# Two decoder layers on one core: the mixers' and the cross attention's input projections get their activations held still and 512 weight columns moved, with the results turned on TensorE

## The chip, the core and the metric

The kernel runs on one core of a Trainium2 chip. The core has a matrix engine (TensorE, "PE" in the profile), a vector engine (VectorE, "DVE"), an activation engine (ScalarE, "ACT"), a general engine (GpSimd, "POOL"), and a synchronisation engine (SyncE, "SP") that here issues nearly all loads. The metric is the time of one execution on the device, in microseconds (us), as the median of several runs.

## The reference

One sequence of 256 tokens, 2048 wide, goes through two decoder layers and a final RMSNorm. All inputs and weights are fp32. Layer 0 has a hybrid mixer, layer 1 a state-space mixer ("ssd"); each is followed by a cross attention into 256 memory tokens and a SwiGLU feed-forward layer 5632 wide. Every part is pre-normed and added to the residual.

```python
def rmsnorm(x, w):
    return x * rsqrt(mean(x * x, -1) + NORM_EPS) * w

def hybrid(p, x):                       # layer 0: one projection 2048 -> 8208, split by columns
    q, f, i, g, qb, kb, vb, gb, beta, a = split(x @ hy_w_in)   # 6 x 1024 of HGRN2/DeltaNet q,k,v, 2 gates, 2 x 8
    o_a = hgrn2_chunked(silu(q), 1 - fg, i, log(fg))           # fg = lb + (1 - lb) * sigmoid(f)
    conv = silu(causal_depthwise_conv([qb, kb, vb], taps=4))
    o_b = gated_delta_chunked(l2norm(q), l2norm(k), v, sigmoid(beta), -exp(a_log) * softplus(a + dt_bias))
    return concat(gated_head_norm(o_a), gated_head_norm(o_b)) @ hy_w_out

def ssd(p, x):                          # layer 1: 2048 -> 10304
    z, xBC, dt = split(x @ ssd_w_in)                           # 4096, 4096 + 2 * 1024, 64
    x, B, C = split(silu(causal_depthwise_conv(xBC, taps=4) + b))
    y = scan over chunks(x * dt, B, C, exp(-exp(a_log) * dt)) + D * x
    return rmsnorm(y * silu(z)) @ ssd_w_out

def xattn(p, x, mem):                   # 4 heads of 128
    q, k, v = x @ xa_wq, norm(mem) @ xa_wk, norm(mem) @ xa_wv
    return softmax(q @ k.T / sqrt(128)) @ v @ xa_wo

def ffn(p, x):
    return (silu(x @ w_gate) * (x @ w_up)) @ w_down
```

The gated delta rule is computed by chunks of 128 tokens here; each chunk and head needs the inverse of a unit lower-triangular matrix.

## The kernel before, in words

**Weights.** Every weight matrix is laid out beforehand as tiles of 128 rows by 1024 numbers (512 KB): two k-tiles of 512 columns. A tile is loaded by SP into `wr` (4 buffers), ACT casts it to fp32r as `wh` (line 156), DVE takes the rest `wl` = `wr` - `wh` (line 124). The activations are split in the same way into `u` tiles hi and lo. A product is then three fp32r matmuls: hi by hi, hi by lo, lo by hi (the helper's line 121 is the line of all matmuls). The norm's gain is put on the activations when they are split; its scale per token, r, is put on the result.

**Two forms of a projection.** `xstat` holds a 128x128 piece of the activations still and moves 512 weight columns past it: per k-tile 2 token halves x 3 matmuls, the result has tokens on the partitions, and r is one number per partition. The gates, the feed-forward layers and all output projections have this form (rows "acc<-wh,u" and "acc<-wl,u", 128x512). `wstat` holds a 128x128 piece of the weights still and moves the 256 tokens: per k-tile 4 x 3 matmuls, the result has channels on the partitions, and r must stand along the free axis, spread over all partitions (`row`, tile `rB`); DVE multiplies the accumulator by it (`scaled`). The mixers' q, k, v, f, x, B, C, z, the attention's q and k, and two blocks of 128 columns that hold the small heads (beta, a, dt) have this form (rows "acc<-u,wh" and "acc<-u,wl", 128x256).

**Around them.** PSUM has 4 banks for accumulators ("acc") and 4 for the rest ("mx"). The causal convolution (`conv`, line 390) reads channels by tokens from a padded SBUF tile `raw`: one ACT product, three DVE multiply-adds. A tag "b2" of 4 SBUF buffers serves short-lived tiles: squares, norm temporaries, the steps of the triangular inverse, the head norm.

**The triangular inverse** of a DeltaNet head group (`gdn`, twice, 4 heads each): after the k-by-kq products DVE makes M, POOL's queue writes it to a DRAM scratch and reads its 16x16 blocks back, DVE inverts these in 15 steps, and the results go through the scratch again into X and XT. Then come three block levels by two chunks on PE, each a product with XT, an ACT copy (line 619), products with X and with XT and a DVE subtraction; then the products with v and M, the state products ("w,D"), and the head norm (`head_norm`: ACT squares, a DVE sum and a DVE reciprocal square root, four DVE products and four transposes per chunk).

**Order.** The program is written in the order of the mathematics. A list scheduler of the compiler, which runs a simulated timeline, sets the order of the instructions on each engine; loads marked `later` keep their written place. A buffer that rotates (4 of "b2", 4 of "acc") makes its next writer wait for the last reader of the one that is 4 back.

**Start.** The first norm (N0) has its hi part made by DVE (line 267) and lo part by DVE (line 127); its squares are made by ACT, added by POOL and DVE, summed over partitions with ones on PE, and `row` is made of that. The residual h (4 tiles of 512 KB) is loaded between the two DeltaNet groups.

Of the kernel before, what the change touches and what calls it, by code (L numbers as in the profile page):

```python
# [9 lines left out]
F32 = mybir.dt.float32  # L10
# [8 lines left out]
P = 128  # L19
# [9 lines left out]
for _name, _w in (("norm_mix", 32), ("norm_xattn", 32), ("norm_mem", 32), ("norm_ffn", 32), ("norm_final", 16),  # L29
                  ("lb", 16), ("hgrn_norm", 8), ("gdn_conv", 96), ("gdn_norm", 8),  # L30
                  ("ssd_conv", 192), ("ssd_conv_b", 48), ("ssd_norm", 32), ("ssd_d", 32),
                  ("gdn_a_log", 1), ("gdn_dt_bias", 1), ("ssd_a_log", 1), ("ssd_dt_bias", 1)):
# [13 lines left out]
    "ssd_w_in": ([(0, KT, n, 512) for n in range(0, 8192, 512)] + [(0, KT, n, 256) for n in range(8192, 10240, 256)]  # L46
# [32 lines left out]
def trunk(ctx: ExitStack, tc: tile.TileContext, A: dict, out: bass.AP):  # L79
# [92 lines left out]
    def wstat(W, n0, n, u, k0=0, nk=KT):  # L172

        nt = n // P
        accs = [pa.tile([P, min(2, nt), T], F32, name="acc", tag="acc") for _ in range((nt + 1) // 2)]
        for k, wh, wl in wtiles(W, k0, nk, n0, n):
            xh, xl = u[k // 4][0][:, k % 4, :], u[k // 4][1][:, k % 4, :]
            for c in range(nt):
                o = accs[c // 2][:, c % 2, :]
                sl = slice(c * P, (c + 1) * P)  # L180
                mm(o, wh[:, sl], xh, k == 0 and c % 2 == 0, False)
                mm(o, wh[:, sl], xl, False, False)
                mm(o, wl[:, sl], xh, False, k == nk - 1)
        return accs
# [29 lines left out]
    class SquareSum:  # L214
# [17 lines left out]
        def rows(self, n):  # L232

            rB = cp.tile([P, T], F32, name="rB", tag="rB", bufs=2)
            ps = psb([P, T])
            mm(ps, ones, self.s)
            rsqrt(rB, ps, n)
            return rB

# [9 lines left out]
    class Norm:  # L249


        def __init__(self, gain, load=None, hi=act):
            self.hi = hi
            self.gain = gain
            self.load = load
            self.u = Lazy(self.loaded) if load else []
            self.ss = SquareSum()
            self.rB = self.r = None

        def block(self, nb, src):  # L260
            hi, lo = utiles()
            for c in range(4):
                g = col(self.gain[0], self.gain[1] + nb * 4 + c)
                if self.hi is act:
                    act.activation(hi[:, c], src[:, c], AF.Copy, scale=g)  # L265
                else:
                    dve.tensor_scalar(hi[:, c], src[:, c], g, None, op0=ALU.mult)  # L267
                stt(lo[:, c], src[:, c], g, hi[:, c].bitcast(F32), ALU.mult, ALU.subtract)
            self.u.append((hi, lo))
            self.ss.add(src)  # L270
            return hi, lo

        def loaded(self, nb):
            self.block(nb, self.load(nb))
            if nb == 3 and self.hi is act:
                self.row()
                self.column()
# [789 lines left out]
```

## Time and profile before

| what | value |
| --- | --- |
| median of 3 runs | 2985.55 us (2983.79 to 2987.41) |
| the profiled execution | 2986.46 us, of which the span from first to last instruction is 2984.4 us |
| PE busy | 2948.9 us (99%), 16970 rows |
| DVE busy | 1808.7 us (61%) |
| ACT busy | 1427.8 us (48%) |
| POOL busy | 308.4 us (10%) |
| mean granted clock of PE | 0.996 |

By the names of the weights in the trace the hybrid mixer lies at 0 to about 600 us, its cross attention to 702, the first feed-forward layer to 1440, ssd to 2165, the second cross attention to 2248, and the second feed-forward layer to the end.

A row of a group reads: line, engine, operation, output<-inputs, shape, xcount | busy us, mean ns of one | idle before, and what ended it. A row of the chain of waits reads: start us, duration us, engine, tile and line, xcount. A row of a table by stretches reads: from:to, length, then busy us (xcount) of PE, weight loads, DVE, ACT and POOL, then the granted clock, the DMA share and GB/s. An fp32 matmul that isn't fp32r stands as two rows of the trace; the order's listings below show it as one.

### The profile page before, as it was taken

How to read it: one execution, taken by the hardware profiler on the slowest of the kernel's cores; microseconds unless marked ns; L12 is line 12 of the kernel's file. 1: busy time of each engine (PE TensorE's matmuls, PEld its weight loads, DVE VectorE, ACT ScalarE, POOL GpSimd, SP SyncE). 2: the span in 40 equal slices, each digit the busy share in tenths (PEclk: the TensorE clock that was granted, in tenths of full speed). 3: DMA queues.
4: the chain of work that ended last, by engine and by line, in shares of the span. 5: the costliest groups of instructions: out<-in, count | busy, mean ns of one | idle time of the engine just before them, and what ended most of it. 6: DMA issues, size and time to landing. Idle time of an engine off the chain costs nothing.

```text
span 2984.4 us, 42629 instructions
## 1 busy us (share of the span) xinstructions
PE 2948.9 (99%) x16970; PEld 2594.9 (87%) x16970; DVE 1808.7 (61%) x2284; ACT 1427.8 (48%) x1809; POOL 308.4 (10%) x257
## 2 busy tenths in 40 slices
PE   8999999999999999999999999999999999999998
PEld 8899898898888888888999989998888888888887
DVE  8777587676455445455677746767675454455455
ACT  5445354555443444344555545555555444443344
POOL 2211232020000000000032302322010000000000
PEclk9999999999999999999999999999999999999999
DMA  6554434555655665655545465545655556666654
GB/s 228 189 158 149 157 114 152 186 192 171 189 190 192 191 192 187 196 189 186 170 156 170 154 193 169 163 163 168 190 193 184 190 190 191 191 190 191 195 188 145
DMA packets 152183, 533.66 MB, mean 179 GB/s; under 512 B 16592, under 2 KB 22864, under 8 KB 151984
## 3 DMA queue, kind: packets, MB, share of 16 engines
q1 hardware_dynamic: 150096, 526.08, 54.9%
q0 software_dynamic: 1472, 4.59, 0.6%
q8 instruction: 133, 2.18, 0.3%
q14 instruction: 66, 0.54, 0.1%
q10 hardware_dynamic: 416, 0.27, 0.0%
HBM read 526.42 MB, written 4.46 MB: 178 GB/s over the span
## 4 chain that ended last, share of the span: by engine, by line
PE 92%; DVE 2%; issue 2%; DMA 1%; ACT 1%; POOL 1%; POOLq 0%; DVEq 0%; SPq 0%; ACTq 0%
PE acc L121 85%; PE mx L121 5%; PE mx L302 1%; DVE wl L124 1%; DMA wr<-in_memT 1%; DMA XT<-scratch 0%; POOL tmp L124 0%; DVE tmp L124 0%; ACT wh L156 0%; DMA scratch<-b 0%; PE mx L902 0%; DVE b L124 0%; DVE u L267 0%; DVE u L127 0%; ACT u L265 0%
## 5 line engine op out<-in xcount | busy, mean ns | idle before, releaser
L124 DVE TENSOR_TENSOR wl<-wr,wh 128x1024 fp32r<-128x1024 f32 x980 | 1240.7, 1268 | 1026.8 <-ACT wh L156 1024.3
L121 PE MATMUL acc<-wh,u 128*128 128x512 f32 (+1 forms) x5728 | 1755.8, 387 | 0.0
L156 ACT CAST wh<-wr 128x1024 fp32r<-128x1024 f32 x980 | 1029.6, 1052 | 1314.3 <-PE acc L121 1203.9
L121 PEld LDWEIGHTS acc<-wh,u 128*128 128x128 f32 x5728 | 1069.6, 188 | 214.4 <-issue 0.2
L121 PE MATMUL acc<-wl,u 128*128 128x512 f32 (+1 forms) x2864 | 1108.3, 387 | 0.0
L121 PE MATMUL acc<-u,wh 128*128 128x256 f32 x4416 | 815.7, 286 | 6.8 <-DVE u L267 6.4
L121 PEld LDWEIGHTS acc<-u,wh 128*128 128x128 f32 x4416 | 696.6, 193 | 11.6 <-ACT wh L156 6.4
L121 PE MATMUL acc<-u,wl 128*128 128x256 f32 x2208 | 628.7, 285 | 4.6 <-DVE wl L124 4.6
L121 PEld LDWEIGHTS acc<-wl,u 128*128 128x128 f32 x2864 | 538.6, 188 | 106.1 <-issue 0.2
L121 PEld LDWEIGHTS acc<-u,wl 128*128 128x128 f32 x2208 | 425.6, 193 | 6.5 <-DVE wl L124 5.3
L396 POOL MEMSET raw<- 128x12 f32 x18 | 2.0, 112 | 1160.4 <-PE mx L302 731.8
L124 POOL TENSOR_TENSOR tmp<-tmp,kq 128x512 f32<-128x512 f32 x32 | 59.7, 1893 | 119.6 <-ACT tmp L700 91.8
L124 POOL TENSOR_TENSOR tmp<-gh,cst 128x512 fp32r<-128x512 f32 x36 | 48.2, 1342 | 102.7 <-PE mx L121 68.5
L124 DVE TENSOR_TENSOR h<-h,acc 128x512 f32<-128x512 f32 (+1 forms) x84 | 52.2, 655 | 9.6 <-PE acc L121 9.4
L127 DVE SCALAR_TENSOR_TENSOR cv<-raw,cols,cv 128x256 f32<-128x256 f32 x120 | 53.1, 500 | 0.0
L127 DVE SCALAR_TENSOR_TENSOR u<-mx,cols,u 128x256 fp32r<-128x256 f32 x96 | 43.0, 478 | 10.5 <-ACT u L323 7.1
L124 POOL TENSOR_TENSOR tmp<-gl,cst 128x512 fp32r<-128x512 f32 x36 | 48.7, 1355 | 1.4 <-DVE gl L124 1.4
L323 ACT ACTIVATE u<-mx,cols 128x256 fp32r<-128x256 f32 x80 | 34.3, 470 | 20.6 <-PE mx L302 17.0
L124 POOL TENSOR_TENSOR ss<-ss,b 128x256 f32<-128x256 f32 x36 | 42.1, 1169 | 1.6
L124 POOL TENSOR_TENSOR b<-b 128x256 f32<-128x256 f32 x36 | 31.1, 881 | 87.3 <-ACT b L224 84.5
L124 DVE TENSOR_TENSOR u<-mx,u 128x512 fp32r<-128x512 f32 x48 | 31.0, 683 | 11.0 <-ACT u L156 11.0
L124 POOL TENSOR_TENSOR MD<-MD,b 128x1536 f32<-128x1536 f32 x8 | 35.1, 4390 | 5.4 <-ACT MD L420 5.4
(278 smaller groups left out, 1369.2 us busy)
## 6 DMA issues: line engine op xcount, KB each, us to landing
wr<-in_ffn_w_gate SPq DMA_DIRECT2D x176, 512.0 KB, 3.5
wr<-in_ffn_w_up SPq DMA_DIRECT2D x176, 512.0 KB, 3.5
wr<-in_ffn_w_down SPq DMA_DIRECT2D x176, 512.0 KB, 3.5
wr<-in_ssd_w_in SPq DMA_DIRECT2D x162, 512.0 KB, 3.5
wr<-in_hy_w_in SPq DMA_DIRECT2D x130, 512.0 KB, 3.6
wr<-in_ssd_w_out SPq DMA_DIRECT2D x64, 512.0 KB, 3.5
wr<-in_hy_w_out SPq DMA_DIRECT2D x32, 512.0 KB, 3.5
wr<-in_xa_wq SPq DMA_DIRECT2D x16, 512.0 KB, 3.4
```

The costliest lines, as they stand in the source:

```text
L121: pe.matmul(o, lhsT=lhsT, rhs=rhs, start=start, stop=stop, skip_group_check=True)
L124: e.tensor_tensor(o, a, b, op=op)
L127: dve.scalar_tensor_tensor(o, a, s, b, op0=op0, op1=op1)
L156: act.copy(hi, src)
L302: pe.transpose(ps[:, x, a * P:(a + 1) * P], src[a][:, c * P:(c + 1) * P], ident)
L323: act.activation(hi[:, c], ps[:, x], AF.Copy, scale=g)
L396: pool.memset(raw[:, 0:n, 0:3], 0.0)
```

## The change

34 blocks of 512 columns go from `wstat` to `xstat`: the 6 of q, k and v and the 4 of f and q in layer 0, x, z, B and C (20) in ssd, and q and k of both cross attentions (4). B and C, which were done in blocks of 256 columns for two groups at a time, are done in blocks of 512 for four. Two functions are new: `rows` evicts the two accumulators on ACT into two "b2" tiles, scaled by r per partition, with an activation function where one is wanted; `turned`, which existed for the residual, transposes them by eight 128x128 transposes into two PSUM banks ("mx"). The convolution, the sigmoids of f and the products with z read these banks; the padded tile, `scaled`, `row` and `rB` are gone. The small heads stay in `wstat` form, are copied and transposed before their functions, and worked on per token. N0's hi part is made by ACT; its r comes from the residual h, loaded early, by eight ACT squares with a sum, and the memory's r of layer 0 is kept for layer 1.

```diff
-    def wstat(W, n0, n, u, k0=0, nk=KT):
+    def wstat(W, n0, u):
...
     class Norm:
-        def __init__(self, gain, load=None, hi=act):
+        def __init__(self, gain, load, r=None):
...
-                if self.hi is act:
-                    act.activation(hi[:, c], src[:, c], AF.Copy, scale=g)
-                else:
-                    dve.tensor_scalar(hi[:, c], src[:, c], g, None, op0=ALU.mult)
+                act.activation(hi[:, c], src[:, c], AF.Copy, scale=g)
                 stt(lo[:, c], src[:, c], g, hi[:, c].bitcast(F32), ALU.mult, ALU.subtract)
...
-        def row(self):
-            if self.rB is None:
-                self.rB = self.ss.rows(D)
-            return self.rB
-
-        def scaled(self, o, acc, n=2):
-            tt(dve, o, acc, self.row().unsqueeze(1).to_broadcast([P, n, T]), ALU.mult)
...
     def turned(src, i):
         ps = psb([P, 2, T])
         for x in range(2):
             c = 2 * i + x
             for a in range(2):
                 pe.transpose(ps[:, x, a * P:(a + 1) * P], src[a][:, c * P:(c + 1) * P], ident)
         return ps
...
-    def conv(c, raw, m, w):
-        act.activation(c, raw[:, m, 3:3 + T], AF.Copy, scale=w[:, 3:4])
-        for i in range(3):
-            stt(c, raw[:, m, i:i + T], w[:, i:i + 1], c, ALU.mult, ALU.add)
+    def conv(c, x, w):
+        act.activation(c, x, AF.Copy, scale=w[:, 3:4])
+        for s in range(1, 4):
+            stt(c[:, s:T], x[:, 0:T - s], w[:, 3 - s:4 - s], c[:, s:T], ALU.mult, ALU.add)
+
+    def rows(N, W, n0, func=AF.Copy, first=None):
+        accs = xstat(W, n0, 512, N.u)
+        if first:
+            first()
+        r = N.column()
+        o = [t4("b2", [P, 512]) for _ in range(2)]
+        for a in range(2):
+            act.activation(o[a], accs[a], func, scale=r[:, a:a + 1])
+            if func == AF.Sigmoid:
+                stt(o[a], accs[a], r[:, a:a + 1], o[a], ALU.mult, ALU.mult)
+        return o
+
+    def columns(N, W, n0, func=AF.Copy):
+        o = rows(N, W, n0, func)
+        return [turned(o, i) for i in range(2)]
+
+    def heads_by_token(N, W, n0, c0):
+        s = t4("w", [P, T])
+        act.copy(s, wstat(W, n0, N.u))
+        ps = psb([P, 2, P])
+        for a in range(2):
+            pe.transpose(ps[:, a], s[:, a * P:(a + 1) * P], ident)
+        return ps[:, :, c0:P]
...
         def conv_in(j, g, o):
-            accs = wstat(W, 4096 + 1024 * j + 512 * g, 512, N.u)
-            if (j, g) == (1, 0):
-                constants_in()
-            raw = padded()
-            for i in range(2):
-                N.scaled(raw[:, 2 * i:2 * i + 2, 3:3 + T], accs[i])
-            for m in range(4):
-                conv(o[:, m, :], raw, m, col("gdn_conv", 4 * (8 * j + 4 * g + m), 4))
+            o_rows = rows(N, W, 4096 + 1024 * j + 512 * g, first=constants_in if (j, g) == (1, 0) else None)
+            ps = [turned(o_rows, i) for i in range(2)]
+            for m in range(4):
+                conv(o[:, m, :], ps[m // 2][:, m % 2], col("gdn_conv", 4 * (8 * j + 4 * g + m), 4))
...
     def xattn(layer, N, nxt):
-        accs = wstat(("xa_wq", layer), 0, 512, N.u)
         q = t4("cv", [P, 4, T])
-        for i in range(2):
-            N.scaled(q[:, 2 * i:2 * i + 2], accs[i])
+        for i, ps in enumerate(columns(N, ("xa_wq", layer), 0)):
+            act.copy(q[:, 2 * i:2 * i + 2], ps)
...
-            accs = wstat(W, 512 * g, 512, N.u)
-            z = t4("gate", [P, 4, T])
-            for i in range(2):
-                N.scaled(z[:, 2 * i:2 * i + 2], accs[i])
-            act.activation(z, z, AF.Silu)
-            tt(dve, y, y, z, ALU.mult)
+            for i, z in enumerate(columns(N, W, 512 * g, AF.Silu)):
+                tt(dve, y[:, 2 * i:2 * i + 2], y[:, 2 * i:2 * i + 2], z, ALU.mult)
...
-    N0 = Norm(("norm_mix", 0), load_x, dve)
+    def input_r():
+        load_h()
+        N = RowNorm(None)
+        for nb in range(4):
+            N.squares(nb, h[nb])
+        return N.column()
+
+    N0 = Norm(("norm_mix", 0), load_x, input_r)
```

The scheduler's order changes with it, at three places that the prediction speaks of. The first is PE during the first triangular inverse (X and XT are the halves of the inverse, b the "b2" tiles of its levels, acc the projections). Before:

```order
L121 MATMUL mx<-X,b_1490 128x128 x4
L121 MATMUL mx<-b_1490,X 128x128 x4
L121 MATMUL mx<-XT,b_1504 128x128 x4
L121 MATMUL acc<-u,wh 128x256 x2
L121 MATMUL acc<-u,wl 128x256
...
L121 MATMUL mx<-X,b_1511 128x128 x4
L121 MATMUL mx<-XT,b_1519 128x128 x4
```

and of the change:

```order
L121 MATMUL mx<-XT,b_1128 128x128 x4
L121 MATMUL mx<-X,b_1135 128x128 x4
L121 MATMUL mx<-b_1135,X 128x128 x4
L121 MATMUL mx<-XT,b_1149 128x128 x4
...
L121 MATMUL mx<-X,b_1234 128x128 x4
L121 MATMUL mx<-vt,X 128x128 x4
L121 MATMUL mx<-w,MD 128x128 x4
L121 MATMUL mx<-vt,X 128x128 x4
L121 MATMUL mx<-w,D 128x128 x12
L429 MATMUL mx<-cst,b_1297 128x128 x3
```

Before, some 26 projection matmuls stood between any two steps of the inverse; now no projection matmul stands between its first step and the head norm's transposes (line 429), in either of the two groups. 157 of 512 columns stand between the last k-by-kq product and the first step, where 358, nearly all of 256 columns, stood; for the second group it is 145 for 329.

The second place is PE in the first cross attention (kq holds the softmax, X and cv are k and q, D and MD the turned softmax). Before, the second half's scores were followed by 20 projection matmuls and then the softmax's transposes; of the change:

```order
L755 MATMUL mx<-cst,kq 128x128 x8
L121 MATMUL mx<-X,cv 128x256 x4
L755 MATMUL mx<-cst,kq 128x128 x8
L121 MATMUL mx<-D,XT 128x256 x2
L121 MATMUL mx<-MD,XT 128x256
```

The scores (X,cv) and their softmax's transposes now stand next to each other. In the second cross attention 32 and 22 projection matmuls still stand ahead of the two sets of transposes.

The third is SP's queue at the start. Of the change:

```order
L165 DMA wr<-in_hy_w_in 128x1024 x4
L111 DMA cst<-in_cst 128x384
L112 DMA cols<-in_cols 128x704
L912 DMA h_84<-in_x 128x2x512
L912 DMA h_85<-in_x 128x2x512
L912 DMA h_86<-in_x 128x2x512
L912 DMA h_87<-in_x 128x2x512
L165 DMA wr<-in_hy_w_in 128x1024 x10
```

The four loads of h stand behind the eighth weight tile and ahead of the ninth, where they stood 27 loads later. ACT's eight squares of h stand, in the same way, ahead of its cast of the ninth tile.

More of the change, by code (lines that the diff above doesn't have):

```diff
@@ L488, in small_heads @@
[L488 to L498 removed]
+            ps = heads_by_token(N, W, 8080, 112)
@@ L764, in load_mem @@
             return raw
-        M = Norm(("norm_mem", 16 * layer), load_mem)
-        accs = wstat(("xa_wk", layer), 0, 512, M.u)
+        M = Norm(("norm_mem", 16 * layer), load_mem, mem_r[0] if mem_r else None)
         k = t4("X", [P, 4, T])
-        for i in range(2):
-            M.scaled(k[:, 2 * i:2 * i + 2], accs[i])
+        for i, ps in enumerate(columns(M, ("xa_wk", layer), 0)):
+            act.copy(k[:, 2 * i:2 * i + 2], ps)
+        if not mem_r:
+            mem_r.append(cp.tile([P, 2], F32, name="mem_r"))
+            dve.tensor_copy(mem_r[0], M.column())
         pT = [t4(tg, [P, 4, T]) for tg in ("D", "MD")]
```

196 lines of the change are left out of this document (65 added, 131 removed).

## The prediction

> **What bounds the kernel now.** First the page's busy times, then its shares of the chain of waits:
>
> ```profile
> PE 2948.9 (99%) x16970; PEld 2594.9 (87%) x16970; DVE 1808.7 (61%) x2284; ACT 1427.8 (48%) x1809; POOL 308.4 (10%) x257
> PE 92%; DVE 2%; issue 2%; DMA 1%; ACT 1%; POOL 1%; POOLq 0%; DVEq 0%; SPq 0%; ACTq 0%
> ```
>
> PE works nearly all the time and the chain runs through it. So the time changes by what PE has to do, and by the few places where PE stands still. The table by stretches (columns: from:to, length, busy PE, weight loads, DVE, ACT, POOL, granted clock, DMA share, GB/s) tells where these are:
>
> ```profile
> 0.00:25.00 25.00, 15.71 (x100) 14.59 (x100) 21.09 (x32) 14.48 (x18) 15.01 (x24) 1.00 0.76 272
> 134.00:215.00 81.00, 79.92 (x675) 79.69 (x674) 52.53 (x96) 32.06 (x39) 15.72 (x19) 1.00 0.54 167
> 1440.00:2165.00 725.00, 725.00 (x5299) 681.35 (x5298) 495.60 (x609) 396.78 (x568) 159.13 (x121) 1.00 0.53 170
> 2165.00:2248.00 83.00, 81.90 (x466) 71.51 (x465) 63.47 (x110) 48.16 (x88) 7.92 (x8) 1.00 0.59 190
> ```
>
> All of ssd (1440 to 2165) is PE at full clock without a gap. The start is not: PE has 15.71 of 25 us. The first triangular inverse (134 to 215) costs PE only 1.1 us, since projections stand between its steps.
>
> **The price of a matmul.** From the chain of waits, in a feed-forward layer (first two rows), in ssd, and at the first norm:
>
> ```profile
> 763.76 0.87 PE mx L302 x8
> 764.64 15.43 PE acc L121 x68
> ...
> 1599.97 26.04 PE acc L121 x217
> ...
> 40.82 0.43 PE mx L121 x2
> ```
>
> The 512-column form takes 15.43/68 = 226.9 ns, the 256-column form 26.04/217 = 120.0 ns, a transpose .87/8 = 109 ns. Two short matmuls cost 240 ns where one long one costs 227.
>
> **Part 1, PE's own work.** A block of 16 k-tiles was 192 short matmuls, 23.04 us, and is 96 long ones, 21.78 us: 1.26 us less, for 34 blocks -42.8 us. Each block adds eight transposes, .87 us: +29.6. The three row sums over a square sum (.43 each), three spreads of r over the partitions (two fp32 matmuls of 128 columns, bounded by the same .43) and four of the small heads' eight transposes (.44) go, with some single-column sums: -3.4. Together **-16.6 us**. The bounds come from the rows' scatter: 1% on the long form's price would be 7.4 us, but the two feed-forward stretches that I divided agree within .1 ns, so +-2.
>
> The Trainium skill, "TensorE: Matmul & The Clock Gate", section "Back-to-back issue gap", gives an isolated gap of N/2.4 + 2.5 ns, 215.8 ns for 512 columns and 109.2 for 256. By it a block would save only .25 us, 34 blocks 8.5 us, and the part would be +17.7 instead of -16.6; the rows above, at 226.9 and 120.0, disagree with the half of it that matters here.
>
> **Part 2, the start.**
>
> ```profile
> 5.32 1.05 ACT wh L156
> ...
> 11.64 3.07 DVE u L267 x4
> ...
> 27.16 13.65 PE acc L121 x92
> ```
> ```profile
> L124 DVE TENSOR_TENSOR wl<-wr,wh 128x1024 fp32r<-128x1024 f32 x980 | 1240.7, 1268 | 1026.8 <-ACT wh L156 1024.3
> ...
> L127 DVE SCALAR_TENSOR_TENSOR u<-mx,cols,u 128x256 fp32r<-128x256 f32 x96 | 43.0, 478 | 10.5 <-ACT u L323 7.1
> ```
> ```profile
> 26.00:28.00 2.00, 0.84 (x4) 0.84 (x5) 2.00 (x4) 0.06 (x1) 0.00 (x0) 0.50 0.00 0
> 28.00:30.00 2.00, 2.00 (x11) 2.00 (x11) 2.00 (x2) 0.00 (x0) 0.00 (x0) 0.50 0.79 252
> ```
>
> DVE makes both halves of the first activations (12.3 us of hi, 16 at .77) and every wl, and PE waits for it; the clock then falls to .50 as well. The first block ends at 40.82 (row above) and is 23.04 us of work: PE lags 17.8 us. Now ACT makes hi. DVE is left with 16 lo parts (.48 us in the group) and eight wl of 1.27: 17.8 us, less than the 21.8 us of the first block, so PE lags by what the first tile takes (cast at 6.4 us) and 2 to 3 us of catching up: 9 to 10. That is -8; I take **-7**, since the squares of h now stand in ACT's queue ahead of the ninth tile's cast. The loads of h (2 MB) and the constants (0.5 MB) take 6.5 us at 385 GB/s (the row at 322 us, below) behind the eighth tile, which is issued when the fourth is split, at about 15 by DVE's work above. So the squares end at about 25, the ninth tile is split at 27, and PE asks for it at about 31. If it comes 6 us later than that, half the gain goes, and more if DVE lags as well: -8.5 to +2.
>
> **Part 3, evictions.**
>
> ```profile
> L124 DVE TENSOR_TENSOR raw<-acc,rB 128x512 f32<-128x512 f32 x44 | 29.9, 688 | 8.2 <-PE acc L121 7.9
> L826 ACT ACTIVATE gate<-acc,r 128x512 f32<-128x512 f32 x16 | 10.8, 689 | 5.9 <-PE acc L121 5.9
> ```
>
> DVE loses two scalings of .69 us a block, ACT gains two evictions of the same length. In ssd this is 27.6 us on ACT: 396.8 + 27.6 of 725, below 60%. PE there has other projections between an eviction and its transposes. So I cost it at the head of PE's queue only, where a transpose comes before its eviction: **+2** (0 to 5) in ssd, +2 (0 to 4) in the HGRN2 groups.
>
> **Part 4, the first inverse.** The chain of waits of before:
>
> ```profile
> 134.46 26.80 PE acc L121 x224
> ...
> 165.27 4.80 DMA scratch<-b
> ...
> 178.48 1.13 PE mx L121 x8
> 179.61 3.46 PE acc L121 x29
> 183.07 2.68 PE mx L121 x24
> ```
>
> Each step hides the copies between its products behind projections, here 29 matmuls (3.46 us). In the new order there are none. Why: the next block's eviction needs two "b2" tiles, and these four rotate through the inverse, so that both finished blocks wait in their four banks. What a step costs uncovered is seen at the end of the second inverse, where before runs dry too (timeline: start, length, engine, line, what, idle before):
>
> ```profile
> 359.97 1.06 PE L121 MATMUL mx<-XT,b 128*128 128x128 f32 x8
> 361.75 1.16 PE L121 MATMUL mx<-X,b 128*128 128x128 f32 x8 [0.73 <-ACT b L619]
> 362.75 1.06 PE L121 MATMUL mx<-vt,X 128*128 128x128 f32 x8
> 364.48 1.16 PE L121 MATMUL mx<-w,MD 128*128 128x128 f32 x8 [0.68 <-ACT w L634]
> 366.42 1.16 PE L121 MATMUL mx<-vt,X 128*128 128x128 f32 x8 [0.78 <-DVE vt L124]
> 367.41 2.84 PE L121 MATMUL mx<-w,D 128*128 128x128 f32 x24
> 375.55 0.61 DVE L127 SCALAR_TENSOR_TENSOR b<-mx,hms,gate 128x128 f32<-128x128 f32 x2
> ```
>
> Eight rows are .89 us of work (2.68/24 each). From XT,b to X,b it is 1.78 us, so .89 of waiting; six such: 5.3. From v,X to w,M 1.73 and on to v,X 1.94: .84 and 1.05, together 1.9. The head norm from the last w,D (about 370.0) to its first product took 5.5 us with a weight split of 1.23 between: 4.4. The clock, after the one longer stall here:
>
> ```profile
> 321.89 1.32 PE L121 MATMUL mx<-XT,b 128*128 128x128 f32 x8 [2.34 <-DMA XT<-scratch]
> ```
> ```profile
> 322.00:324.00 2.00, 2.00 (x11) 1.81 (x12) 0.00 (x0) 0.59 (x1) 0.64 (x1) 0.67 1.02 385
> 324.00:326.00 2.00, 2.00 (x7) 1.52 (x5) 0.00 (x0) 0.00 (x0) 0.64 (x1) 0.50 0.54 213
> 366.00:368.00 2.00, 1.58 (x14) 1.58 (x15) 0.36 (x1) 0.39 (x1) 0.00 (x0) 1.00 0.00 0
> ```
>
> 2.34 us of standing cost .66 + 1.0 = 1.7 us of clock, the short gaps none. The head norm's 4.4 us gives one such loss. So 5.3 + 1.9 + 4.4 + 1.7 - 1.1 = **+12.2** (lower bound 8, if the head norm overlaps the next block and the clock holds; upper bound 18, if the scratch's trip, 178.48 - 134.46 = 44.0 us, is no longer covered by 157 x .227 = 35.6 us and some of that 8 us shows).
>
> The Trainium skill, the same page, section "What's actually happening", has the clock fall after an idle window of about 3.4 us. By it the 2.34 us stall should have cost nothing, but the trace has .50 behind it; by the page the terms of 1.7 us for the 4.4 us gaps stay.
>
> **Part 5, the second inverse.** The same 13.3, less what it costs before: 2.34 + 1.7 + .89 + 1.9 = 6.8. **+6.5** (2 to 12).
>
> **Part 6, the cross attentions.**
>
> ```profile
> 662.57 1.84 PE acc L121 x8
> ...
> 666.96 1.04 PE L794 MATMUL mx<-cst,kq 128*128 128x128 f32 x8
> ```
>
> From the second scores' end (662.5) to their transposes (666.96) 20 projection matmuls cover 4.4 us of softmax. They are gone in the first attention: 4.4 + 1.7 of clock, **+6.1** (3 to 7). In the second the 1.1 us of PE's idle time (row 2165:2248) can go: **-1**.
>
> **The sum**: -16.6 - 7 + 2 + 2 + 12.2 + 6.5 + 6.1 - 1 = +4.2 us. One more stall, with its clock, lay behind DVE's scalings of the first blocks and goes (.49 + 1.0): +2.7.
>
> ```profile
> 88.00:90.00 2.00, 1.51 (x14) 1.51 (x14) 0.98 (x1) 2.00 (x7) 0.00 (x0) 1.00 0.03 2
> ...
> 92.00:94.00 2.00, 2.00 (x11) 2.00 (x11) 1.97 (x6) 1.04 (x1) 2.00 (x2) 0.50 0.34 59
> ```
>
>  On the profiled execution's 2986.46 (span 2984.4 and 2.06 around it) this gives 2989.2; that execution lies .9 above the median of the runs shown, so on the median 2985.55 + 2.7 = **2988.3 us**.
>
> **The rivals.**
>
> *A: the gaps cost less than priced* (faster). PE starts a head norm's transposes as soon as the first head is ready, the copies on ACT are no longer behind casts, and the start gives all 8.5. For it: ACT and DVE have nothing else to do while PE stands. Against: the order has nothing to fill in. Inverses at 8 + 2, attention 3, start -8.5, the rest as above: -16.6 - 8.5 + 2 + 10 + 3 - 1 - 1.5 = -12.6: 2973.
>
> *B: the scratch's trip becomes the wait* (slower). DVE's 15 inversion steps and the two trips need their 44 us whatever PE does; PE runs out of the two blocks it may hold in its four banks before X is back, in both groups, and stands with the clock at .50. It decides once the trip is longer than 35.6 us (32.9 for the second group, 145 matmuls). Price: up to 8 + 1.7 more in each: 2988.3 + 10 to 19, about 3002. For it: both trips before were longer. Against: DVE has fewer things to do in the meantime, and some accumulations lie ahead on PE's queue when the M products reach DVE.
>
> *C: ACT becomes the bound* (slower) in the mixers, through 68 evictions of .69 us (46.9) and the table loads that new switches of functions bring: if half of the 46.9 us shows, 2988.3 + 23.4 = 3012. Against: ACT at 55% in ssd.
>
> *D: long matmuls gain nothing over two short ones*, in these stretches: without the 42.8 us it is 3031. Against: the two rows of price. By the skill's gap it would be 34 us, not 42.8.
>
> **Chances.** Forecast .48, A .25, B .18, C .05, D .02, and .02 that the change does in effect nothing. A run of this kernel can tell about .2%, 6 us, from no change: faster is below 2979.6, slower above 2991.5. Within the forecast (its own range 2981 to 2997) .28 falls to no change, .18 to slower and .02 to faster. So faster .26, same .33, slower .41. The range, leaving out a part of A and of B, and C and D: 2972 to 3003.
>
> **What would show it.** In the profile after: mean ns of long matmuls in ssd as in the feed-forward layers, and PE's total some 17 us lower by work; the first matmul after the first block at about 31 us instead of 40.8; at each inverse a run of 16 steps in which PE stands .7 to .9 us before every second one, then 4 to 5 us behind the head norm, and a clock below 1 after it; in the first attention 4 us before the second set of transposes. I am wrong if PE's idle time outside the inverses and the first attention grows by more than 5 us (evictions), or if PE stands for XT by more than 3 us (B).

## The result, and the profile after

The changed kernel takes 3000.53 us (2998.11 to 3001.31, 4 runs) where the kernel before takes 2984.67 us (2982.31 to 2987.41, 4 runs): slower, ratio 1.0051 with the interval 1.0034 to 1.0069, or 15.9 us. The forecast was 2988.3 with a range of 2972 to 3003. The two profiled executions stand 11.65 us apart (2986.46 and 2998.11, spans 2984.4 and 2996.3), since the one of before lies above its median and the other below; the lengths below are of these. First the busy times and the chain's shares of the page after:

```profile
PE 2944.5 (98%) x13948; PEld 2450.2 (82%) x13948; DVE 1735.7 (58%) x2154; ACT 1486.4 (50%) x1916; POOL 262.7 (9%) x209
PE 94%; DMA 2%; DVE 1%; ACT 1%; issue 1%; POOL 0%; DVEq 0%; SPq 0%; ACTq 0%; POOLq 0%
```

PE has less work, but the span is 11.9 us longer: PE stands more. What it waits for, by sum, count and longest (us), before:

```profile
PE acc L121 <- DVE u L267: 6.4, 1, 6.4
PE acc L121 <- DVE wl L124: 4.6, 2, 3.5
PE mx L121 <- DMA XT<-scratch: 3.4, 2, 2.3
```

and after:

```profile
PE mx L121 <- ACT b L585: 8.6, 12, 0.7
PE mx L429 <- DVE b L127: 8.3, 2, 4.2
PE acc L121 <- ACT wh L156: 7.0, 2, 6.6
PE mx L121 <- DMA XT<-scratch: 4.9, 2, 3.9
PE mx L755 <- DVE kq L751: 4.6, 1, 4.6
```

The start's waits on DVE are gone (6.6 us for the first tile stay). In their place stand twelve waits for a copy in the two inverses, two of 4.2 us for the head norms, one of 4.6 us for the first softmax. The length of each stretch, measured between the last rows of turnings of the residual h on PE (lines 302 and 278) at its two ends; the last column shares the terms of the forecast's sum out to the stretches:

| stretch | before | change | start alone (e4) | forecast for the change |
| --- | --- | --- | --- | --- |
| layer 0's mixer | 595.4 | 612.3 (+16.9) | 582.0 (-13.4) | about +6 |
| first attention | 106.6 | 110.6 (+4.0) | 108.8 (+2.2) | +5 |
| first feed-forward | 731.0 | 731.1 | 731.2 | 0 |
| ssd | 709.4 | 705.3 (-4.1) | 709.2 | -6 |
| second attention | 104.6 | 100.6 (-4.0) | 103.6 (-1.0) | -2 |
| second feed-forward | 737.4 | 736.4 | 736.5 | 0 |

These borders cut through work, since PE begins an attention's projections before the last turning ahead of it. In the traces 29 short matmuls of the first attention and 41 of the second stand ahead of the border where the attention has short blocks, 23 and 29 long ones where it has long blocks: 3.5 and 4.9 us against 5.2 and 6.6. So 1.7 us of the mixer's +16.9 belong to the first attention, and ssd's stretch holds 1.7 us more of the second. Put where they belong, the changes are +15.2, +5.7, -5.8 and -2.3.

The sizes fit everywhere but in layer 0's mixer. There, the chain of waits after, in the first and the second inverse:

```profile
161.84 1.14 PE mx L121 x8
163.01 0.59 ACT b L585
163.65 2.96 PE mx L121 x24
166.67 0.59 ACT b L585
...
288.63 5.34 DMA scratch<-b
294.25 7.05 DMA XT<-scratch
301.44 2.06 PE mx L121 x8
303.52 0.59 ACT b L585
304.16 5.50 PE mx L121 x24
```

A copy of .59 us now stands between every two groups of PE, and the same 24 rows that take 2.96 us in the first inverse take 5.50 in the second. The table by stretches says why (columns as before):

```profile
300.00:304.00 4.00, 2.05 (x8) 1.78 (x8) 0.00 (x0) 0.48 (x1) 0.36 (x1) 0.50 0.82 273
304.00:308.00 4.00, 3.84 (x18) 3.84 (x19) 0.01 (x1) 0.11 (x1) 0.90 (x1) 0.50 0.01 3
308.00:312.00 4.00, 3.28 (x22) 2.99 (x22) 1.27 (x2) 0.58 (x1) 1.26 (x1) 0.78 0.00 0
```

After a wait of 3.93 us for XT, up to 301.44, the granted clock is .50 and then .78: half of 2.6, half of 4 and .22 of 4 us, together 4.2 us, are lost while PE works.

### The profile page after: what moved, and what is told of

It reads as the page before. It is cut to its first block, busy times and chain, and to the rows that moved or that the text cites. A ratio compares the mean times of both kernels' runs of the same rounds, so it can differ in the third digit from the quotient of the medians.

```text
span 2996.3 us, 36590 instructions
## 1 busy us (share of the span) xinstructions
PE 2944.5 (98%) x13948; PEld 2450.2 (82%) x13948; DVE 1735.7 (58%) x2154; ACT 1486.4 (50%) x1916; POOL 262.7 (9%) x209
## 4 chain that ended last, share of the span: by engine, by line
PE 94%; DMA 2%; DVE 1%; ACT 1%; issue 1%; POOL 0%; DVEq 0%; SPq 0%; ACTq 0%; POOLq 0%
PE acc L121 86%; PE mx L121 6%; PE mx L278 2%; DMA XT<-scratch 0%; DVE wl L124 0%; DMA scratch<-b 0%; POOL tmp L124 0%; DMA wr<-in_memT 0%; DMA b<-scratch 0%; ACT b L585 0%; PE mx L850 0%; DMA scratch<-MD 0%; DVE b L124 0%; PE mx L429 0%; DMA wr<-in_hy_w_in 0%
## 5 line engine op out<-in xcount | busy, mean ns | idle before, releaser
L121 PE MATMUL acc<-wh,u 128*128 128x512 f32 (+1 forms) x7904 | 2450.4, 390 | 7.0 <-ACT wh L156 7.0
L121 PEld LDWEIGHTS acc<-wh,u 128*128 128x128 f32 x7904 | 1480.1, 188 | 305.2 <-ACT wh L156 7.8
L121 PE MATMUL acc<-wl,u 128*128 128x512 f32 (+1 forms) x3952 | 1536.5, 389 | 1.3 <-DVE wl L124 1.3
L121 PEld LDWEIGHTS acc<-wl,u 128*128 128x128 f32 x3952 | 744.4, 188 | 150.8 <-DVE wl L124 2.9
L127 DVE SCALAR_TENSOR_TENSOR cv<-mx,cols,cv 128x255 f32<-128x255 f32 (+2 forms) x120 | 52.5, 475 | 13.6 <-ACT cv L351 13.0
L363 ACT ACTIVATE b<-acc,r 128x512 f32<-128x512 f32 x66 | 43.9, 687 | 27.0 <-PE acc L121 16.9
L278 PE MATMUL mx<-cst,b 128*128 128x128 f32 x272 | 39.1, 274 | 0.0
L124 DVE TENSOR_TENSOR X<-X,mx 128x512 f32<-128x512 f32 x28 | 18.5, 683 | 32.9 <-PE mx L121 32.9
L278 PEld LDWEIGHTS mx<-cst,b 128*128 128x128 f32 x272 | 32.3, 141 | 5.9 <-issue 1.4
L121 PE MATMUL mx<-tmp,mr 128*128 128x512 f32 x108 | 32.7, 406 | 0.0
L121 PEld LDWEIGHTS mx<-tmp 128*128 128x128 f32 x240 | 28.8, 196 | 2.5 <-POOL tmp L124 1.9
```

Source lines behind the costliest of these rows:

```text
L121: pe.matmul(o, lhsT=lhsT, rhs=rhs, start=start, stop=stop, skip_group_check=True)
L124: e.tensor_tensor(o, a, b, op=op)
L127: dve.scalar_tensor_tensor(o, a, s, b, op0=op0, op1=op1)
L278: pe.transpose(ps[:, x, a * P:(a + 1) * P], src[a][:, c * P:(c + 1) * P], ident)
L363: act.activation(o[a], accs[a], func, scale=r[:, a:a + 1])
```

## The experiments

Each was timed beside the kernel before on the same chip, whose median there was 2988 to 2990 us; "below" and "above" are by these. Kernels "with stationary weights" use the old form (`wstat4`, 512 columns at a time) with r spread over the partitions (`scaled`), on the changed kernel.

### Own tiles for the evicted rows (e1)

```diff
-        o = [t4("b2", [P, 512]) for _ in range(2)]
+        if tag:
+            o = t4(tag, [P, 2, 512])
+            o = [o[:, 0], o[:, 1]]
+        else:
+            o = [t4("b2", [P, 512]) for _ in range(2)]
...
```

The tag is "cv" for DeltaNet's q and for HGRN2's f and q, "raw" for DeltaNet's k and v: tiles of 4 KB that are free at that time. ssd and the attentions stay on "b2".

> Layer 0's evicted rows go to tiles of their own (tags of 4 KB that are free at that time) in place of two of the four b2 tiles; nothing else is changed. The order now has 22 to 24 projection matmuls between the steps of the first inverse, none in the second. Theory 1 (the evictions wait for b2 tiles that rotate through the inverse, so finished blocks keep the four accumulator banks and PE runs dry): the first inverse costs no more than before the change, the second stays uncovered; about 14 us less than the change, 2986 to 2988 us. Rival (PE runs dry for the trip through the scratch, or for the clock, whatever the tiles): within 4 us of the change, 2997 to 3003 us.

3003.65 us (3003.0 to 3007.59), ratio 1.0055 [1.0042, 1.0068], 14.9 above: no better than the change. But the theory didn't simply fall. The chain of waits at the first inverse, and PE's waits:

```profile
162.53 1.13 PE mx L121 x8
163.66 5.47 PE acc L121 x24
169.12 2.68 PE mx L121 x24
171.80 5.00 PE acc L121 x22
```
```profile
PE mx L121 <- DMA XT<-scratch: 12.7, 2, 11.1
PE mx L433 <- DVE b L127: 8.4, 2, 4.2
```

The first inverse's steps are covered again, and PE works through them without a stop; the head norm behind them stays open (4.2 us), so some 8 of the 14 us come back. What was won there is lost at the second inverse, where PE now waits 11.05 us for XT instead of 3.93, and in the HGRN2 groups behind it, where it waits 4.8 us for POOL's `tmp` instead of 1.8. The projections that fill the first inverse are those that would have stood ahead of the second. The "b2" tiles were the cause of the first gap, not of the loss as a whole.

### Layer 0's mixer with stationary weights (e2)

```diff
-            o_rows = rows(N, W, 4096 + 1024 * j + 512 * g, ...)
+            accs = wstat4(W, 4096 + 1024 * j + 512 * g, N.u)      # and so for f and q
```

> The ten blocks of layer 0's mixer go back to stationary weights and 256 moving columns, scaled by a row of r that is spread from the new r; the new start, the small heads by token, ssd and both attentions stay as changed. Theory 1 (the loss of the change lies in the mixer of layer 0 past its start, some 26 us in the profile after, and in the first attention, 5; start, ssd and second attention gain about 9, 4 and 4): 2970 to 2976 us. Rival (the start's gain is given back at the first inverse, since that has its own length through the scratch, and ssd gains nothing): 2982 to 2990 us.

2971.63 us (2969.38 to 2972.17), ratio 0.9942 [0.993, 0.9955], 17.2 below. The mixer is 584.3 us long instead of 612.3: its ten long blocks cost 28 us, where my sum had 12.2 + 6.5 + 2 - 10 x .39 = 16.8.

### The attentions with stationary weights (e3)

```diff
-        for i, ps in enumerate(columns(N, ("xa_wq", layer), 0)):
-            act.copy(q[:, 2 * i:2 * i + 2], ps)
+        accs = wstat4(("xa_wq", layer), 0, N.u)                   # and so for k
+        for i in range(2):
+            scaled(N, q[:, 2 * i:2 * i + 2], accs[i])
```

> The q and k blocks of both attentions go back to stationary weights; all else as changed. Theory 1 (the missing cover of the first softmax costs 6 us, and the second attention gains 4 by other things than the form, such as the kept r of the memory): 6 us less than the change, 2993 to 2996 us. Rival (the two attentions nearly cancel, as the profile's landmarks have it, +5 and -4, both by the form): within 2 us of the change, 2998 to 3002 us.

3000.05 us (2998.37 to 3001.34), ratio 1.0038 [1.0024, 1.0051], 11.3 above. By medians 4 us less than the change, with intervals that overlap. The stretches decide for the rival, though not by its sizes: the second attention is 103.6 us instead of 100.6, the first 111.9 instead of 110.6. The softmax's wait did go from 4.55 to 1.0 us, but others came: 2.0 us for a sum of squares on POOL, and more work in the short blocks. With the work at the borders counted where it belongs (ssd's stretch is 703.7 us here against 705.3), the form of the second attention is worth 1.3 us, not 3.

### The start alone (e4)

As e2 and e3 together, and ssd in the old form as well:

```diff
-            for i, z in enumerate(columns(N, W, 512 * g, AF.Silu)):
-                tt(dve, y[:, 2 * i:2 * i + 2], y[:, 2 * i:2 * i + 2], z, ALU.mult)
+            accs = wstat4(W, 512 * g, N.u)                            # and so for x, B and C
+            z = t4("gate", [P, 4, T])
+            for i in range(2):
+                scaled(N, z[:, 2 * i:2 * i + 2], accs[i])
+            act.activation(z, z, AF.Silu)
+            tt(dve, y, y, z, ALU.mult)
```

> All 34 blocks go back to stationary weights; what is left of the change is the start (hi by ACT, r from the early loaded h), the small heads by token, r spread from the per-token r, and the kept r of the memory. Theory 1 (DVE was the bound of the first 30 us, and the 8 to 9 us won there stay won): 2974 to 2977 us. Rival (what is won at the start is waited for later, at the first inverse or for the weights behind the load of h): 2982 to 2986 us.

2973.12 us (2972.45 to 2976.23), ratio 0.9951 [0.9939, 0.9964], 15.7 below. All of the gain stays, and more than the 8 to 9 us of the start. On top comes the second inverse: PE waits .89 us there for XT where it waited 2.34, and the clock stays at 1.00 behind it, which with the 1.7 us of slow clock that are gone makes some 3 us. Of the -3.4 us for the row sums only about 1.3 is left here, since r is spread six times (24 rows of PE) where the kernel before spread it three times.

### Long form only where no chain needs cover (e5)

As e2, and in the first attention only:

```diff
-        for i, ps in enumerate(columns(N, ("xa_wq", layer), 0)):
-            act.copy(q[:, 2 * i:2 * i + 2], ps)
+        if layer:
+            for i, ps in enumerate(columns(N, ("xa_wq", layer), 0)):
+                act.copy(q[:, 2 * i:2 * i + 2], ps)
+        else:
+            accs = wstat4(("xa_wq", layer), 0, N.u)                   # and so for k
...
```

> Long matmuls only where no serial chain needs cover: ssd and the second attention as changed, the ten mixer blocks of layer 0 and the first attention's q and k with stationary weights; the new start. Theory 1 (a chain that is hidden by projections loses its cover where their blocks are long, in the first attention some 5 us): 5 us below the kernel with layer 0's mixer short, so 21 to 23 us below the kernel before. Rival (the first attention loses nothing by its form; with both attentions short the time stayed within .5 us): 16 to 18 us below.

2969.99 us (2968.3 to 2973.33), ratio 0.994 [0.9927, 0.9952], 18.2 below, at the rival's edge. The first attention, with short blocks, is 111.1 us long, .7 less than in e2 with long ones, and the mixer's stretch 2.4 less, of which 1.7 is the attention's work ahead of the border. By the profiles that is 3.2 us together, by the medians 1 to 2: less than the 5 of the theory, and not the rival's nothing.

### One more tile for HGRN2 (e6)

```diff
-            fs = t4("raw", [P, 4, T])
-            for i, ps in enumerate(columns(N, W, 1024 + 512 * g, tag="cv")):
+            for i, ps in enumerate(columns(N, W, 1024 + 512 * g, tag="raw")):
...
-                act.activation(fs[:, 2 * i:2 * i + 2], ps, AF.Sigmoid, scale=-1.0)
+                act.activation(kq[:, 0, 2 * i:2 * i + 2], ps, AF.Sigmoid, scale=-1.0)
```

> As with own tiles, but HGRN2's two evicted blocks get one 4 KB tile each (the sigmoid of -f is written to its destination, so the third tile is free). The order now has 150 instead of 98 projection matmuls ahead of the second inverse, and 22 between its first steps. Theory 2 (the stock of finished or open blocks, four accumulator banks and the free eviction tiles, is the cover; where own tiles only moved it from the second inverse to the first, two more tiles add to it): the second inverse's 11 us wait for the scratch becomes 3 or less, 12 to 16 us below the kernel with own tiles, 0 to 3 us above the kernel before. Rival (the cover is moved again, to the work behind): within 4 us of the kernel with own tiles, 11 to 15 us above before.

The edit is shown against e1. 2987.57 us (2984.94 to 2989.84), ratio 0.9997 [0.9988, 1.0006], .7 below before and 16 below e1. One more 4 KB tile does that:

```profile
PE mx L121 <- POOL tmp L124: 6.4, 3, 2.3
...
PE mx L433 <- DVE b L127: 4.2, 1, 4.2
PE mx L121 <- ACT b L590: 2.9, 4, 0.7
PE mx L121 <- DMA XT<-scratch: 2.5, 2, 1.4
```

The waits for XT are 2.5 us instead of e1's 12.7, one head norm is covered, and four copies are left open. The rival has a part of it: PE waits 6.4 us for POOL's `tmp` in the HGRN2 groups behind, where the change waits 1.8, so a part of the cover did move.

### HGRN2's f and q with stationary weights (e7)

```diff
-            for i, ps in enumerate(columns(N, W, 1024 + 512 * g)):
+            accs = wstat4(W, 1024 + 512 * g, N.u)                     # and so for q
...
```

> Only HGRN2's f and q blocks (four) go back to stationary weights; the six convolution blocks and all else stay as changed, on the two b2 tiles. They are the cover of the second inverse: 289 short matmuls stand ahead of it in the order, 26 and 15 after its first two steps; the first inverse is as in the change. Theory 2 (half of the loss lies at the second inverse, in the wait for the scratch with its slow clock): 10 to 16 us below the change, 0 to 5 us above the kernel before. Rival (the loss belongs to the first inverse and the convolutions, or is the transposes' own): within 5 us of the change, 11 to 17 us above before.

2996.89 us (2992.58 to 3005.43), ratio 1.0028 [1.0019, 1.0037], 8.7 above: between the two, 4 us less than the change in the mixer's stretch (608.3). The wait for XT fell from 3.93 to .98 us and the slow clock at 300 to 312 us went with it, but most steps of the second inverse, both head norms and the whole first inverse stay open. So that wait with its clock was some 7 of the second inverse's 15 us, and two covered steps gave 1.8 more. Nearly 4 went again behind the second head norm: PE waits 1.2 us for DVE's scaling, which the short form brings back, and the clock stands at .50 for some eight us, where the change has .63 for four and .94 for the next four:

```profile
330.00:334.00 4.00, 3.23 (x12) 2.32 (x12) 3.77 (x13) 2.16 (x5) 0.00 (x0) 0.50 0.02 4
334.00:338.00 4.00, 3.58 (x9) 2.81 (x9) 1.85 (x5) 3.92 (x5) 0.00 (x0) 0.50 0.00 0
```

And four short blocks are 4 x .39 = 1.6 us longer than four long ones.

### Only the hi part on ACT (e8), only r early (e9)

```diff
-                if self.hi is act:
-                    act.activation(hi[:, c], src[:, c], AF.Copy, scale=g)
-                else:
-                    dve.tensor_scalar(hi[:, c], src[:, c], g, None, op0=ALU.mult)
+                act.activation(hi[:, c], src[:, c], AF.Copy, scale=g)
```

> The kernel before with one edit: the hi part of the first norm is made by ACT, not by DVE; r still comes from the squares of x and the row sums. Theory 3 (DVE was the bound of the start, and its 12 us of hi parts are the whole gain): 7 to 9 us below the kernel before. Rival (the early r from h, which takes the squares' additions off POOL and DVE, is the larger part of the 15.7 us that the start alone gave): 0 to 4 us below.

2984.9 us (2984.36 to 2990.87), ratio 0.9994 [0.9985, 1.0003], 3.3 below, with an interval that includes no change: the rival. So the other half was tried, the start alone with hi back on DVE:

```diff
-                act.activation(hi[:, c], src[:, c], AF.Copy, scale=g)
+                if self.gain == ("norm_mix", 0):
+                    dve.tensor_scalar(hi[:, c], src[:, c], g, None, op0=ALU.mult)
...
```

> The start alone (all 34 blocks with stationary weights), but the hi part of the first norm back on DVE; r still comes early from h, so POOL adds no squares. Theory 3 (POOL's additions slow DVE's two-input instructions, .64 to .96 us a lo part beside them and .48 without, and that is most of the start's gain; hi on DVE costs .34 each without POOL): 16 x (.34 + .48) + 8 x 1.22 = 23 us of DVE for the first block's 23 us of PE, so 2 to 4 us above the start with hi on ACT, 11 to 14 us below the kernel before. Rival (DVE's own work bounds the start, by the number of its instructions): most of the gain goes, 3 to 8 us below the kernel before.

2974.62 us (2972.37 to 2975.8), ratio 0.9948 [0.9935, 0.9962], 14.9 below, as much as both together (15.7). DVE's groups in the first 30 us, of e8 (POOL adds squares) and of e9 (it doesn't):

```profile
L124 DVE TENSOR_TENSOR wl<-wr,wh 128x1024 fp32r<-128x1024 f32 x8 | 11.2, 1415 | 0.6 <-ACT wh L156 0.6
L127 DVE SCALAR_TENSOR_TENSOR u<-XT,cols,u 128x256 fp32r<-128x256 f32 x4 | 3.6, 962 | 0.0
```
```profile
L124 DVE TENSOR_TENSOR wl<-wr,wh 128x1024 fp32r<-128x1024 f32 x9 | 10.8, 1218 | 0.0
L127 DVE SCALAR_TENSOR_TENSOR u<-XT,cols,u 128x256 fp32r<-128x256 f32 x4 | 1.8, 477 | 0.0
L267 DVE TENSOR_SCALAR u<-cv,cols 128x256 fp32r<-128x256 f32 x4 | 1.2, 349 | 4.5 <-DMA cv<-in_xT 4.5
```

The same instruction takes 962 ns beside POOL's additions and 477 without them. DVE's hi parts at .35 us each then fit beside PE. The gain of the start is the early r, by what it takes from POOL. (e9 keeps e4's other parts, the small heads by token and the memory's r; its gain at the start itself is as large as e4's.) The Trainium skill, "SBUF — State Buffer", section "Who interferes with whom", states that the port pair that VectorE and GpSimd share is the only contention between engines, and an exclusive lock. The two fences agree: the lo part, which reads two tensors of SBUF, lasts twice as long.

### Own tiles and short f and q (e10)

The edit of e1 for the convolution blocks, and that of e7:

```diff
-        o = [t4("b2", [P, 512]) for _ in range(2)]
+        if tag:
+            o = t4(tag, [P, 2, 512])
+            o = [o[:, 0], o[:, 1]]
+        else:
+            o = [t4("b2", [P, 512]) for _ in range(2)]
...
-            for i, ps in enumerate(columns(N, W, 1024 + 512 * g)):
+            accs = wstat4(W, 1024 + 512 * g, N.u)
```

> Own tiles for the six convolution blocks and stationary weights for HGRN2's f and q. The order now covers the first inverse with 22 to 24 long matmuls a step, but has 66 short ones (8 us) ahead of the second and none in it, where the kernel with only HGRN2 short had 289 (35 us). Theory 2 (the time lost is the trip through the scratch, some 37 us, less the projections that stand ahead of it, and the stock of these is shared by both inverses): the first inverse gives 14 us, the second waits 25 to 29 us more for the scratch, so 10 to 20 us above the kernel with HGRN2 short, 18 to 28 us above before. Rival (the trip is as long as DVE and the queues are busy, and shortens where PE asks early): the gain of the first stays, 4 to 8 us below before.

3009.32 us (3005.59 to 3010.13), ratio 1.0061 [1.0048, 1.0073], 19.8 above. Two edits that each helped or did no harm are together the slowest:

```profile
PE mx L121 <- DMA XT<-scratch: 21.7, 2, 20.0
```

Theory 2 has the sign and nearly the size (19.95 us of waiting, 16 to 19 more than the kernels beside it, where 25 to 29 were expected). That the total still lies in its range is partly luck: the first inverse gave back some 8 us, not 14, since its head norm stays open. For six kernels, the projections ahead of the second inverse (from the order, times the price of one) and the wait for XT:

| kernel | projections ahead | us | wait for XT | together |
| --- | --- | --- | --- | --- |
| before | 242 short, 87 long | 48.8 | 2.34 | 51.1 |
| change | 145 long | 32.9 | 3.93 | 36.8 |
| e1 | 98 long | 22.2 | 11.05 | 33.3 |
| e6 | 150 long | 34.0 | 1.17 | 35.2 |
| e7 | 289 short | 34.7 | .98 | 35.7 |
| e10 | 66 short | 7.9 | 19.95 | 27.9 |

The trip isn't a constant: from the kernel before to the change it shrinks by 14 us where 16 us of projections are taken from beside it, and to e10 by 9 more where 25 more are taken, so that part of e10's rival is true. The wait is what the projections leave of it.

### ssd alone (e11), the attentions alone (e12)

On e4, ssd's blocks in the changed form:

```diff
-            accs = wstat4(W, 512 * g, N.u)
...
+            for i, z in enumerate(columns(N, W, 512 * g, AF.Silu)):
+                tt(dve, y[:, 2 * i:2 * i + 2], y[:, 2 * i:2 * i + 2], z, ALU.mult)
```

> The start alone and the twenty blocks of ssd in long form; layer 0's mixer and both attentions with stationary weights. Theory (a long block saves 1.26 - .87 = .39 us of PE's time, 7.8 for ssd, and the evictions cost some 2 to 4 of it back; no serial chain stands in ssd): ssd's stretch 4 to 6 us shorter than with the start alone, 19 to 22 us below the kernel before. Rival (transposes and evictions eat the gain): within 2 us of the start alone, 14 to 17 us below before.

2968.19 us (2967.0 to 2971.56), ratio 0.9939 [0.9925, 0.9952], 20.0 below: the lowest median of this study (e5's runs overlap with it). ssd's stretch is 703.7 us against 709.2 with the start alone, -5.5.

On e4, the attentions' q and k in the changed form:

```diff
-        accs = wstat4(("xa_wq", layer), 0, N.u)
...
+        for i, ps in enumerate(columns(N, ("xa_wq", layer), 0)):
+            act.copy(q[:, 2 * i:2 * i + 2], ps)
```

> The start alone and the four blocks of the two attentions in long form; both mixers with stationary weights. Theory (the first attention's second softmax loses its cover of 4.4 us by the long form, the second attention gains 3): the first attention's stretch 3 to 5 us longer than with the start alone, the second's 3 us shorter, 13 to 17 us below the kernel before. Rival (the first attention's length is set by the order that the scheduler finds for the stretch as a whole, since two kernels with short blocks there had 109 and 111 us): its stretch within 2 us of the start alone, 17 to 20 us below before.

2977.01 us (2975.11 to 2983.58), ratio 0.9967 [0.9955, 0.9978], 11.2 below, so some 4 us above the start alone, but only part of that lies in the attentions: the first is 110.1 us against 108.8, the second 100.6 against 103.6. The missing cover is there as forecast,

```profile
PE mx L795 <- DVE kq L791: 4.6, 1, 4.6
```

where the start alone waits 1.0 us, and yet the stretch is only 1.3 us longer: a wait of 1.0 us for POOL's sum of squares is not there in turn, and its two blocks have less work. Layer 0's mixer and ssd are longer by 2.3 and 1.7 us as well, though nothing in them was edited: 1.7 us of each is the attention's own long matmuls ahead of the border, as in the table by stretches. So the form costs 3.0 us in the first attention, at the theory's lower edge, and gives 1.3 in the second. The change costs 5.7 us in the first attention; 2.2 of that are in the start alone too, with short blocks, and belong to the order, which the scheduler makes anew with each edit.

## Why the prediction was right, and where it was off

The range held and the sign was the likeliest of the three; the point was 12 us low. The time came out where rival B had it (about 3002), and by the prediction's own sign its forecast is wrong in one place: PE stands for XT by more than 3 us (3.93). So the range held because a part of B was left inside it, not because the point's sum was right. The two profiled executions differ by 11.9 us where the sum has 2.7, and all of the 9 us between lie in layer 0's mixer, where the term of the second inverse alone was 8 to 10 us short. Below, "time lost" is PE's time less its matmuls at their prices (120, 227 and 109 ns as above, 112 ns for a row of 128 fp32 columns), so both standing and slow clock. By the steps:

- **Part 1, PE's own work: right.** In ssd after, the chain has a row of 62 long matmuls in 14.09 us, 227 ns each, as in the feed-forward layers. With nothing else changed, ssd's twenty blocks gave 5.5 us (e11).
- **Part 2, the start: right in size, wrong in cause.** The time lost in the first 120 us fell by 8 to 9 us in the start alone; I had 7 + 1.5. But I counted DVE's instructions at their slow durations and gave the gain to the hi parts, so that the size fits is luck. The sixteen hi parts took 8.2 us before, not 12.3: two tiles at .34 to .35 us an instruction, and two at .74 to .85. Moving the hi parts alone gives 3 us, not clear of none (e8); taking the additions from POOL gives nearly all (e9). The row that could have told it was quoted: 3.07 us for four hi parts, .77 each, beside POOL at 15 of 25 us. The late ninth tile didn't come.
- **Part 3, evictions: right in size, not in cause.** In ssd 7.8 us were expected from the blocks and 5.5 came, so 2.3 were left over; I had 2. But PE doesn't stand in ssd after at all:

```profile
1451.00:2159.00 708.00, 708.00 (x3416) 582.05 (x3414) 464.37 (x569) 422.25 (x602) 138.94 (x103) 1.00 0.54 170
```

So nothing there waits for an eviction. In the traces of e4 and e11 most of the 2.3 us lie in the spacing of matmuls next to the transposes: the last transpose of a row and the long matmul behind it often take some 343 ns where their prices sum to 336, and the long ones next to it 230 to 236 ns instead of 227. The reason for that isn't shown. In the HGRN2 groups the time lost rose by 2.0 us, as I had it, but 1.2 of that is a longer wait for POOL's `tmp` (1.8 us instead of .6), no eviction.
- **Part 4, the first inverse: right.** Twelve waits of .7 us in the two inverses, 4.17 us for the head norm, a clock of .50 (194 to 196 us) and .86 (196 to 200) behind it, .92 us for XT: the terms nearly as I took them, together 14 us for 12.2. e1 shows the cause I gave, the "b2" tiles, since other tiles bring the cover back.
- **Part 5, the second inverse: the term that was mis-sized.** I took the first inverse's 13.3 us for it and left the trip through the scratch to the upper bound of part 4 and to rival B. The trip took 36.8 us where 32.9 us of projections stood: 3.93 us of waiting and 4.2 us of clock. With the 13.3 that is 21.4, less the 6.8 of before: +15 instead of +6.5; the time lost went from 7.1 to 23.3 us, +16. This is rival B, in the second group alone; e6 and e7, which put more projections ahead of it, lose the wait, and e1 and e10, which put fewer, multiply it. B's reason doesn't hold, though: the trip doesn't need its 44 us whatever PE does, it shrank from 51.1 to 36.8.
- **The mixer as a whole.** The ten long blocks cost 28 us (e2). Against e2 the change loses 15.5 us more at the first inverse, 18.9 at the second (e2 loses only 4.4 there) and 2.3 behind it, and some 4 less ahead of the inverses; less 3.9 of PE's work that is the 28 us within 1.
- **Part 6, the attentions: the wait right (4.55 us for 4.4), its effect in part.** The first attention costs 5.7 us where I had about 5, but only 3.0 of them by the long form (e12): a stall that is seen in a row replaces others. In the second, PE's idle time of 1.1 us, which I let go, stays; the 2.3 us that it gave are less work.

Rival A (gaps that cost less) and C (ACT as the bound) didn't come: ACT is at 50%. D is refuted by the price in ssd. The three chances at the end don't follow from the lines ahead of them, which add up to .27, .30 and .43; nothing rests on that.

## What to carry to other kernels

A matmul form that is some per cent cheaper is worth having where nothing but PE's work sets the time (ssd), and can cost many times that beside a serial chain: there the projections are cover, and each block that needs an eviction and a tile for it before it is out of the way can wait for the very buffers that the chain is using. So count, ahead of a serial chain, how many matmuls can run before every accumulator and every eviction tile is taken, and compare their time with the chain's; a freed 4 KB tile was worth 16 us here. And test the parts of a change apart: the start alone was 15.7 us faster, the long blocks of ssd 4 more, and the ten blocks of the mixer hid both.

## What was not expected of the hardware

Beside POOL's tensor additions, DVE's two-input instructions at the start took 642 to 962 ns instead of 477, its weight splits 1415 instead of 1218. The one-input hi parts took 740 to 846 ns beside them instead of 349. After a stall of 3.93 us the clock stayed at .50 while PE ran short fp32 groups with gaps, for about eight microseconds; after 11.05 us (e1) and 19.95 us (e10) for about six, and three to four after a stall of 2.34 us in full work. So a longer stall didn't make the slow clock longer. A gap of .7 us every few microseconds cost no clock in the first inverse (1.00 from 162 to 190 us).
